# When an attention's value products are issued: one pair of heads at a time, or several pairs together

## The chip, the cores and the metric

The kernel runs on one core of one Trainium2 chip. The metric is the device time in microseconds (us) of one execution. Before the change it is 994.13 us, the median of three runs between 993.94 and 994.28.

## The reference

Two layers of a hybrid decoder work on 256 tokens of width 1024 in float32. Each layer is a gated feed-forward block, a token-mixing block, and a second feed-forward block, each followed by a layer norm of `ALPHA * x + block(x)`. The mixing block projects `x` once, feeds three mixers with the columns (a short convolution, a spatial-gating MLP, and an attention with three branches), and sends the joined results through one output projection. The change touches the attention alone:

```python
# 8 heads of 64 in 2 groups; 256 tokens; three branches with keys and values of their own
o_cmp = softmax(q kc^T, causal on 15 compressed blocks) @ vc
o_s   = softmax(q ks^T, causal) @ vs        # 16 >= 4 blocks: all of them are selected
o_w   = softmax(q kw^T, causal, window 512) @ vw
o     = g0 * o_cmp + g1 * o_s + g2 * o_w    # sigmoid gates per token and head
```

## The kernel before

TensorE products in float32 are split in three: an operand is held as a rounded part ("hi") and a remainder ("lo"), and `hi*hi + hi*lo + lo*hi` is summed in PSUM (`mm3`, L183 to L187, and `proj_chan`, L189 to L197). Weights stream from HBM in blocks of 512 KB and are split on arrival by ScalarE (L162) and VectorE (L163).

The attention part of `mixing` (from L627) goes through twelve steps: four for token tile 0 (128 tokens, one pair of heads each) and eight for token tile 1 (one head each, over 256 keys). A step is
- `scores` (L661 to L674): products of queries and keys of both branches into one PSUM bank, tag `y`, which has 4 slots;
- `attend` (L676 to L702): the maximum (VectorE, L681), the exponentials (ScalarE, L685), their scaling by gate and sum (VectorE, L689 to L692) into a tile `P`, four transposes on TensorE (L696, tile `trp`, tag `tr`, 2 slots), and a copy into `PT` (ScalarE, L698). `P` and `PT` share the tag `a` with 9 slots;
- `values(t, j)` (L704 to L721): for pair `j` of heads, products of the values and `PT` into `o[t]` (L717). `o[t]` is a bank of tag `y` as well. An instruction loads 64 columns of weights (two heads share the 128 output partitions); a float32 product is two instructions, so a pair is 8 of them for tile 0 and 16 for tile 1.

`compressed(t)` (L632 to L659) adds the compressed branch to `o[t]`: eight small instructions (L636, PSUM tile `sc`, tag `tr`), a softmax on VectorE and ScalarE (L641 to L651), a transpose (L653, tile `trc`, tag `tr`), a copy (L655) and 16 instructions of 64 columns (L658), which stand behind the opening products of `values`. `heads_out(t)` (L723) splits the finished `o[t]` into `mixh` and `mixl` for the output projection `w_out`, whose PSUM tiles are `yo`.

Work of the other mixers is written between the steps, to fill TensorE: `conv_h` behind step 0, `spatial` behind step 2 (L570, tile `psv`, also with 64 columns of weights), `conv_c` and `conv_b` behind step 4; `w_out(0)` follows the loop, then `heads_out(1)`, the layer norm of tile 0 and `w_out(1)`.

The order in which it is written is not the order in which it runs. A planner lays out the queue of each engine when the program is compiled: among the instructions that it holds ready at a moment of its own estimate, the one written first goes first, so what is written later fills holes. A tile takes a slot of its tag when the planner places the first instruction that writes it. The engines then work through their queues in that order.

The loop, as it stands before (L734 to L749):

```python
for i, (t, slots) in enumerate(steps):
    if t not in o:
        gates(t)
        o[t] = ps.tile([128, 4, 128], F32, name="o", tag="y", bufs=4)
    for j in range(i and i + 2, min(i + 3, len(steps))):
        sc[j] = scores(*steps[j])
    attend(t, slots, sc.pop(i))
    if slots[-1] % 2:
        values(t, slots[-1] // 2)
    if i in (1, 5):
        compressed(t)
    if i == 3:
        heads_out(0)
    for fn in fill.get(i, []):
        fn()
```

Of the kernel before, what the change touches and what calls it, by code (L numbers as in the profile page):

```python
# [121 lines left out]
def _build(tc, A, out):  # L122
# [3 lines left out]
    with ExitStack() as es:  # L126
# [178 lines left out]
        def layer_norm(t, y, coef, eps, gb, last=False, after=None):  # L305
            g, b = gb
            with tc.high_priority(offset=200):
                st = sm.tile([128, 2, 6], F32, name="st")
                for h in range(2):
                    c = slice(h * 512, h * 512 + 512)  # L310
                    DVE.scalar_tensor_tensor(x[t][:, c], x[t][:, c], coef, y[h], ALU.mult, ALU.add)
                    DVE.bn_stats(st[:, h, :], x[t][:, c])
                mean, rs = rstd_of(st, eps)
                for h in range(2):
                    c = slice(h * 512, h * 512 + 512)
                    DVE.scalar_tensor_tensor(x[t][:, c], x[t][:, c], mean, g[:, c], ALU.subtract, ALU.mult)
                    DVE.scalar_tensor_tensor(x[t][:, c], x[t][:, c], rs, b[:, c], ALU.mult, ALU.add)
                    if last:
                        SP.dma_start(out[t * 128:(t + 1) * 128, c], x[t][:, c])
                    elif after:  # L320
                        with tc.issue_after(after[h].ins):
                            to_xT(t, h)
                    else:
                        to_xT(t, h)
# [121 lines left out]
        def mixing(l, sp):  # L446
# [162 lines left out]
            def w_out(t, kbs, tag, bufs, by_half):  # L609
                w = blocks((l, "wo"))  # L610
                if t not in yo:
                    yo[t] = [ps.tile([128, 512], F32, name="yo", tag=tag, bufs=bufs) for _ in range(2)]
                todo = [(kb, n) for kb in kbs for n in range(2)]
                if by_half:
                    todo.sort(key=lambda v: v[1])
                for kb, n in todo:
                    s = slice(n * 512, n * 512 + 512)
                    mm3(yo[t][n], (mixh[t][:, kb, :], mixl[t][:, kb, :]),
                        (w[kb][0][:, s], w[kb][1][:, s]), kb == 0, kb == 7)
# [7 lines left out]
            def gates(t):  # L627
                e1[t] = sm.tile([128, 3, 8], F32, name="e1")
                ACT.activation(e1[t].rearrange("p a b -> p (a b)"), vv[t][:, 256:280], AF.Exp, scale=-1.0)
                DVE.tensor_scalar(e1[t], e1[t], 1.0, None, op0=ALU.add)  # L630
# [30 lines left out]
            def scores(t, slots):  # L661

                nk = t + 1
                w = nk * 128
                sc = ps.tile([128, 4 // nk, w], F32, name="scm", tag="y", bufs=4)
                for i, s in enumerate(slots):
                    j, g = divmod(s, 2)
                    lq = QS[j // 2][:, j % 2, g, t * 128:t * 128 + 128]
                    dst = sc[:, 2 * i:2 * i + 2, :]
                    PE.matmul(dst, lhsT=lq, rhs=KH[:, g, :, :w], start=i == 0, stop=True, skip_group_check=True)  # L670
                    PE.matmul(dst, lhsT=lq, rhs=KL[:, g, :, :w], start=False, stop=True, skip_group_check=True)
                PE.matmul(sc[:, :, w - 128:], lhsT=identb, rhs=causal[:, :4 // nk, :], start=False, stop=True,
                          skip_group_check=True)
                return sc  # L674

            def attend(t, slots, sc):  # L676
                nk = t + 1
                w = nk * 128
                m = 4 // nk
                nm = sm.tile([128, 4], F32, name="nm")  # L680
                DVE.tensor_reduce(nm[:, :m], sc, AX.X, ALU.max, negate=True)  # L681
                P = wk.tile([128, m, w], F32, name="P", tag="a")
                su = sm.tile([128, 4], F32, name="su")
                for i in range(m):
                    ACT.activation(P[:, i, :], sc[:, i, :], AF.Exp, bias=nm[:, i:i + 1], accum_out=su[:, i:i + 1])  # L685
                h = len(slots)
                suv = su[:, :m].rearrange("p (s b) -> p s b", s=h)
                ev = e1[t][:, 1:3, slots[0]:slots[0] + h].rearrange("p b s -> p s b")
                DVE.tensor_tensor(suv, suv, ev, ALU.mult)  # L689
                DVE.reciprocal(su[:, :m], su[:, :m])  # L690
                for i in range(m):
                    DVE.tensor_scalar(P[:, i, :], P[:, i, :], su[:, i:i + 1], None, op0=ALU.mult)  # L692
                Pv = P.rearrange("p a b -> p (a b)")
                tr = ps.tile([128, 4, 128], F32, name="trp", tag="tr")
                for i in range(4):
                    PE.transpose(tr[:, i, :], Pv[:, i * 128:i * 128 + 128], ident)  # L696
                PT = wk.tile([128, 4, 128], F32, name="PT", tag="a")
                ACT.copy(PT, tr)  # L698
                for si, s in enumerate(slots):
                    for br in range(2):  # L700
                        for kb in range(nk):
                            weights[t, s, br, kb] = PT[:, (si * 2 + br) * nk + kb, :]  # L702

            def values(t, j):  # L704

                with ExitStack() as order:
                    for i in opened.get(t, []):  # L710
                        order.enter_context(tc.issue_after(i.ins))
                    for br in range(2):
                        for kb in range(t + 1):
                            for g in range(2):
                                c0 = br * 128 + g * 64
                                first = len(opened.setdefault(t, [])) < 2
                                i = PE.matmul(o[t][half[g], j, :], lhsT=vv[kb][:, c0:c0 + 64],  # L717
                                              rhs=weights.pop((t, 2 * j + g, br, kb)), start=first, stop=True,
                                              skip_group_check=True)
                                if first:  # L720
                                    opened[t].append(i)  # L721

            def heads_out(t):  # L723
                split_to(mixh[t][:, 4:8, :], mixl[t][:, 4:8, :], o[t])
# [5 lines left out]
            with ExitStack() as order:  # L730
                for i in gelus:
                    order.enter_context(tc.issue_after(i.ins))
                sc = {}
# [4 lines that stand above are left out]
                    for j in range(i and i + 2, min(i + 3, len(steps))):  # L738
                        sc[j] = scores(*steps[j])
                    attend(t, slots, sc.pop(i))  # L740
                    if slots[-1] % 2:
                        values(t, slots[-1] // 2)
                    if i in (1, 5):
                        compressed(t)
                    if i == 3:
                        heads_out(0)
                    for fn in fill.get(i, []):
                        fn()
                w_out(0, range(4), "gu", 2, False)  # L749
                w_out(0, range(4, 8), "gu", 2, True)  # L750
                heads_out(1)
                layer_norm(0, yo[0], ALPHA, EPS, gbn)
                w_out(1, range(8), "y", 4, True)
                layer_norm(1, yo[1], ALPHA, EPS, gbn)

        for l in range(L):
            small = []
            ffn(l, 1, 0, mid=lambda: small.append(load_small(l)))
            mixing(l, small[0])
            ffn(l, 2, 2, last=l == L - 1)  # L760
# [37 lines left out]
```

## Time and profile before

| what | value |
|---|---|
| median of the runs | 994.13 us |
| the profiled execution's own time | 993.1 us |
| its span | 991.4 us |
| TensorE busy (PE) | 978.0 us, 99% |
| weight loads (PEld) | 887.4 us, 90% |
| VectorE busy (DVE) | 603.2 us, 61% |
| ScalarE busy (ACT) | 468.4 us, 47% |
| mean granted TensorE clock | 0.997 of full speed |

The own time of the profiled execution holds 1.7 us outside the span. The attention of the first layer lies at about 238 to 300 us of the span, that of the second at about 726 to 789 us. In a row of the timeline the first number is the start, the second the time until the last of the merged instructions ended; since products overlap in the pipeline, what a product costs is read from the distance of starts, not from its own length.

### The profile page before, as it was taken

How to read it: one execution, taken by the hardware profiler on the slowest of the kernel's cores; microseconds unless marked ns; L12 is line 12 of the kernel's file. 1: busy time of each engine (PE TensorE's matmuls, PEld its weight loads, DVE VectorE, ACT ScalarE, POOL GpSimd, SP SyncE). 2: the span in 40 equal slices, each digit the busy share in tenths (PEclk: the TensorE clock that was granted, in tenths of full speed). 3: DMA queues.
4: the chain of work that ended last, by engine and by line, in shares of the span. 5: the costliest groups of instructions: out<-in, count | busy, mean ns of one | idle time of the engine just before them, and what ended most of it. 6: DMA issues, size and time to landing. Idle time of an engine off the chain costs nothing.

```text
span 991.4 us, 16634 instructions
## 1 busy us (share of the span) xinstructions
PE 978.0 (99%) x6824; PEld 887.4 (90%) x6828; DVE 603.2 (61%) x830; ACT 468.4 (47%) x658; POOL 19.7 (2%) x42
## 2 busy tenths in 40 slices
PE   7999999999999999999999999999999999999996
PEld 6999999899878899999889999998988789999995
DVE  6655455686769555455584545548678785545534
ACT  6644444256655444344354444434565663534420
POOL 1000000010000000000000000000000000000000
PEclk9999999999999999999999999999999999999998
DMA  8967565385226666556375766554642265755601
GB/s 284 331 241 237 171 198 187 105 309 160 87 86 194 231 213 194 189 189 205 94 231 195 255 205 202 196 157 168 237 149 85 86 229 198 253 190 184 205 16 42
DMA packets 53067, 183.17 MB, mean 185 GB/s; under 512 B 6656, under 2 KB 7168, under 8 KB 52992
## 3 DMA queue, kind: packets, MB, share of 16 engines
q1 hardware_dynamic: 52992, 182.12, 55.2%
q8 instruction: 53, 0.87, 0.4%
q14 instruction: 22, 0.18, 0.1%
HBM read 181.05 MB, written 1.05 MB: 184 GB/s over the span
## 4 chain that ended last, share of the span: by engine, by line
PE 99%; DMA 0%; DVE 0%; issue 0%; SPq 0%; DVEq 0%; ACT 0%
PE y L185 8%; PE y L187 8%; PE y L186 8%; PE pu L195 7%; PE pg L195 7%; PE pg L197 7%; PE pu L197 7%; PE pg L196 7%; PE pu L196 7%; PE pc L195 3%; PE pc L197 3%; PE pc L196 3%; PE pg L187 2%; PE yo L187 2%; PE yo L185 2%; PE pg L185 2%
## 5 line engine op out<-in xcount | busy, mean ns | idle before, releaser
L163 DVE TENSOR_TENSOR lo<-raw,hi 128x1024 fp32r<-128x1024 f32 (+2 forms) x326 | 389.9, 1203 | 283.1 <-ACT hi L162 267.3
L162 ACT CAST hi<-raw 128x1024 fp32r<-128x1024 f32 (+2 forms) x326 | 335.1, 1037 | 385.6 <-PE pu L196 153.6
L195 PE MATMUL pu<-xTh,hi 128*128 128x256 f32 x576 | 161.3, 280 | 0.0
L195 PE MATMUL pg<-xTh,hi 128*128 128x256 f32 x576 | 161.3, 280 | 0.0
L197 PE MATMUL pu<-xTh,lo 128*128 128x256 f32 x576 | 160.8, 279 | 0.0
L197 PE MATMUL pg<-xTh,lo 128*128 128x256 f32 x576 | 160.8, 279 | 0.0
L196 PE MATMUL pu<-xTl,hi 128*128 128x256 f32 x576 | 160.8, 279 | 0.0
L196 PE MATMUL pg<-xTl,hi 128*128 128x256 f32 x576 | 160.7, 279 | 0.0
L185 PE MATMUL y<-hi,hTh 128*128 128x512 f32 x352 | 138.6, 394 | 0.0
L187 PE MATMUL y<-hi,hTl 128*128 128x512 f32 x352 | 137.4, 390 | 0.0
L186 PE MATMUL y<-lo,hTh 128*128 128x512 f32 x352 | 136.9, 389 | 0.0
L195 PEld LDWEIGHTS pu<-xTh,hi 128*128 128x128 f32 x576 | 108.1, 188 | 1.1
L196 PEld LDWEIGHTS pu<-xTl,hi 128*128 128x128 f32 x576 | 107.8, 187 | 1.1
L197 PEld LDWEIGHTS pu<-xTh,lo 128*128 128x128 f32 x576 | 108.3, 188 | 0.0
L197 PEld LDWEIGHTS pg<-xTh,lo 128*128 128x128 f32 x576 | 108.3, 188 | 0.0
L195 PEld LDWEIGHTS pg<-xTh,hi 128*128 128x128 f32 x576 | 108.1, 188 | 0.1
L196 PEld LDWEIGHTS pg<-xTl,hi 128*128 128x128 f32 x576 | 107.8, 187 | 0.1
L187 PEld LDWEIGHTS y<-hi,hTl 128*128 128x128 f32 x352 | 66.0, 188 | 14.7
L186 PEld LDWEIGHTS y<-lo,hTh 128*128 128x128 f32 x352 | 66.1, 188 | 12.6
L185 PEld LDWEIGHTS y<-hi,hTh 128*128 128x128 f32 x352 | 66.1, 188 | 12.3
L195 PE MATMUL pc<-xTh,hi 128*128 128x256 f32 x256 | 73.0, 285 | 0.0
L197 PE MATMUL pc<-xTh,lo 128*128 128x256 f32 x256 | 72.5, 283 | 0.0
(153 smaller groups left out, 1246.4 us busy)
## 6 DMA issues: line engine op xcount, KB each, us to landing
raw<-in_ws SPq DMA_DIRECT2D x312, 512.0 KB, 4.6
w<-in_ws SPq DMA_DIRECT2D x8, 512.0 KB, 6.1
lng<-in_ln SPq DMA_DIRECT2D x6, 512.0 KB, 6.7
lnb<-in_ln SPq DMA_DIRECT2D x6, 512.0 KB, 7.5
raw<-in_ws SPq DMA_DIRECT2D x8, 256.0 KB, 4.0
raw<-in_ws SPq DMA_DIRECT2D x4, 420.0 KB, 3.5
x<-in_x SPq DMA_DIRECT2D x4, 256.0 KB, 4.5
out<-x SPq DMA_DIRECT2D x4, 256.0 KB, 2.1
```

What stands on the lines that cost most here:

```text
L162: splits.append((ACT.copy(hi, raw), DVE.tensor_tensor(lo, raw, hi.bitcast(F32), ALU.subtract)))
L163: DVE.tensor_tensor(lo, raw, hi.bitcast(F32), ALU.subtract)))
L185: PE.matmul(o, lhsT=a[0], rhs=b[0], start=start, stop=False)
L186: PE.matmul(o, lhsT=a[0], rhs=b[1], start=False, stop=False)
L187: return PE.matmul(o, lhsT=a[1], rhs=b[0], start=False, stop=stop)
L195: PE.matmul(p[:, b, :], lhsT=hi, rhs=xTh[:, k, :], start=k == 0, stop=False)
L196: PE.matmul(p[:, b, :], lhsT=hi, rhs=xTl[:, k, :], start=False, stop=False)
L197: PE.matmul(p[:, b, :], lhsT=lo, rhs=xTh[:, k, :], start=False, stop=k == KC - 1)
```

## The change

Inside the loop, `values` no longer follows each finished pair. The four pairs of token tile 0 are all issued behind step 3, pairs 0 and 1 of token tile 1 behind step 7, and pairs 2 and 3 behind step 11. `compressed(t)` moves behind them: from step 1 to step 3 for tile 0, from step 5 to step 7 for tile 1. Nothing else changes.

```diff
                     attend(t, slots, sc.pop(i))
-                    if slots[-1] % 2:
-                        values(t, slots[-1] // 2)
-                    if i in (1, 5):
+
+
+                    for j in {3: range(4), 7: range(2), 11: range(2, 4)}.get(i, ()):
+                        values(t, j)
+                    if i in (3, 7):
                         compressed(t)
                     if i == 3:
                         heads_out(0)
```

## Rows read from the trace of the kernel before

**Rows 1.** The page: busy time of the engines; the chain that ended last.

```profile
PE 978.0 (99%) x6824; PEld 887.4 (90%) x6828; DVE 603.2 (61%) x830; ACT 468.4 (47%) x658; POOL 19.7 (2%) x42
...
PE 99%; DMA 0%; DVE 0%; issue 0%; SPq 0%; DVEq 0%; ACT 0%
```

**Rows 2.** Timeline, PE: a pair of tile 0; start, length, engine, line, shape, count.

```profile
255.69 0.28 PE L196 MATMUL pc<-xTl,hi 128*128 128x256 f32 x1
255.90 0.66 PE L717 MATMUL o<-PT,vv 128*64 128x128 f32 x8
...
256.71 0.28 PE L195 MATMUL pc<-xTh,hi 128*128 128x256 f32 x1
```

**Rows 3.** Timeline, PE: compressed branch and a pair of tile 0, back to back.

```profile
260.75 1.09 PE L658 MATMUL o<-pcT,vcb 128*64 128x128 f32 x16
261.68 0.61 PE L717 MATMUL o<-PT,vv 128*64 128x128 f32 x8
```

**Rows 4.** Timeline, PE: the transposes of one step between products of the convolution.

```profile
268.57 0.28 PE L195 MATMUL pc<-xTh,hi 128*128 128x256 f32 x1
268.69 0.60 PE L696 MATMUL trp<-ident,P 128*128 128x128 f32 x4
...
269.25 0.28 PE L197 MATMUL pc<-xTh,lo 128*128 128x256 f32 x1
```

**Rows 5.** Timeline, PE: most of a pair of tile 1 between products of `w_out`.

```profile
290.42 0.40 PE L187 MATMUL yo<-hi,mixl 128*128 128x512 f32 x1
290.74 1.09 PE L717 MATMUL o<-PT,vv 128*64 128x128 f32 x14
...
292.10 0.39 PE L186 MATMUL yo<-lo,mixh 128*128 128x512 f32 x1
292.33 0.39 PE L187 MATMUL yo<-hi,mixl 128*128 128x512 f32 x1
```

**Rows 6.** Timeline, PE: the first two instructions of tile 1's first pair.

```profile
271.76 0.41 PE L696 MATMUL trp<-ident,P 128*128 128x128 f32 x2
272.10 0.43 PE L717 MATMUL o<-PT,vv 128*64 128x128 f32 x2
272.47 0.63 PE L636 MATMUL sc<-kcb,qf 128*128 128x32 f32 x4
```

**Rows 7.** Timeline, PEld: the first weight load behind the pair of rows 2.

```profile
256.49 0.19 PEld L197 LDWEIGHTS pc<-xTh,lo 128*128 128x128 f32 x1 [0.17 <-issue]
```

**Rows 8.** Timeline, PE: the first pair of tile 0, and scores behind it.

```profile
250.87 0.66 PE L717 MATMUL o<-PT,vv 128*64 128x128 f32 x8
251.46 0.38 PE L670 MATMUL scm<-KH,QS 128*128 128x256 f32 x1
```

**Rows 9.** Timeline, ACT: the copy of step 0, and the first exponential of step 1.

```profile
249.75 0.59 ACT L698 COPY PT<-trp 128x512 f32<-128x512 f32 x1 [1.39 <-PE trp L696]
250.23 0.37 ACT L685 ACTIVATE P<-scm,nm 128x128 f32<-128x128 f32 x1
```

**Rows 10.** Timeline, PE: spatial products and step 0's transposes, between two convolution products.

```profile
247.46 0.28 PE L197 MATMUL pc<-xTh,lo 128*128 128x256 f32 x1
...
248.03 0.44 PE L696 MATMUL trp<-ident,P 128*128 128x128 f32 x2
...
249.64 0.87 PE L570 MATMUL psv<-wst,vg 128*64 128x128 f32 x10
...
250.66 0.28 PE L196 MATMUL pc<-xTl,hi 128*128 128x256 f32 x1
```

**Rows 11.** Timeline, DVE: compressed branch of tile 0, first and last; convolution, last two.

```profile
255.22 0.29 DVE L641 TENSOR_TENSOR pcm<-sc,cadd 128x128 f32<-128x128 f32 x1
...
258.93 0.28 DVE L651 TENSOR_TENSOR pcm<-pcm,csum 128x128 f32<-128x128 f32 x1
...
269.49 0.48 DVE L596 SCALAR_TENSOR_TENSOR yc<-z,taps,yc 128x254 f32<-128x254 f32 x1
...
271.53 0.68 DVE L602 TENSOR_TENSOR yc<-yc,pc 128x512 f32<-128x512 f32 x1
```

## The prediction, written before the result

> **What bounds the kernel now.** I read the page first: TensorE is busy for 99% of the span and the chain that ended last is TensorE for 99% too [rows 1]. So a microsecond is won only where TensorE does less, or where its queue loses less between two products; making VectorE or ScalarE faster, or their steps earlier, is worth nothing unless TensorE stands still for them. Then I read TensorE's timeline through the attention of layer 1. It has no long idle stretch: low-priority products fill every hole. But starts are not evenly spaced. Where an instruction with 64 weight columns (L717, L658, L570) follows one with 128, and again on the way back, starts come later than the stream's rhythm. That toll is what the change can lower. The same code runs once per layer, so everything below counts twice.
>
> **The price of a switch.** Products of the convolution start 0.12 us apart (268.57 to 268.69) [rows 4]. Behind the one at 255.69 the next two were due at 255.81 and 255.93; the second came at 256.71 [rows 2]. So a group of eight costs 0.78 us. Sixteen instructions of the kind take 261.68 - 260.75 = 0.93, or 0.058 each, and a further group of the same shape behind them pays no toll [rows 3]; eight are 0.46, and 0.32 is the switch. Between products of `w_out`, 0.23 apart, fourteen cost 292.10 - 290.88 = 1.22 (due: 290.42 + 2 x 0.23), less 0.81: 0.41 [rows 5]. Two instructions between transposes and small scores cost 272.47 - 271.76 - 2 x 0.058 = 0.59, less 0.12: 0.47 [rows 6]. A switch there and back is 0.32 to 0.47 us. Four transposes, which have 128 columns, cost 269.25 - 268.81 = 0.44 with a toll of only 0.21 [rows 4].
>
> [...]
>
> **What the change does to the order.** Written order is not queue order, so first the groups before, counted along the timeline of a layer: tile 0 has four (8, 8, 16+8 with the compressed branch, 8), tile 1 eight (2, 14, 16+2, 14, 2, 14, 2, 14). Tile 1's pairs are split because the first product needs only the first head's `PT`, and the planner issues it at once. This is the weak point of the change: `values` is still written ahead of `conv_c`, `conv_b` and `w_out`, which fill TensorE at that time, so a ready pair still goes before them, alone. Written together is not issued together.
>
> One thing holds the pairs back: the PSUM slot of `o[t]`. Tiles of one tag get their slots in the order of their first instructions. Two rows show it. The scores of step 3 start at 251.46, right behind the first pair [rows 8], although step 0's score bank was free before its transposes began at 248.03 [rows 10] and although products of lower priority ran meanwhile: `o[0]`, first written by that pair, stood ahead of them. And the exponentials of step 1 start at 250.23, right behind the copy of step 0 [rows 9], though ScalarE had idled 1.39 us before that copy: `PT` is ahead of the next `P`. Behind the change `o[0]` is first written behind step 3, so the scores of steps 3, 4 and 5 take their slots first, and `o[0]` gets that of step 2, when step 2's exponentials end. These follow the copy of step 1. By then pairs 0 and 1 are ready and go as one group of 16; pairs 2 and 3 and the compressed branch come one after another: 16, 8, 8, 16, again four groups. `o[1]` now stands behind the scores of step 9 and gets its slot behind the exponentials of step 6: both heads of pair 0 are ready then, so its split goes: 16, 2, 14, 16+2, 14, 2, 14, seven groups for eight.
>
> **The sum.**
> - Tile 1, one switch less, the one at 272.10: -0.47 a layer [rows 6]. Bounds: -0.32 (the cheapest row) to -0.94 (if one more pair closes up), nothing if the slot comes early. I take the row of that group itself.
> - Tile 0, value groups: none. Bounds: 0.32 either way, for one group more or less.
> - Scores of step 3 are free of `o[0]` now and stand right behind `conv_h`, those of step 4 behind them: both before `spatial` in priority. Before, `spatial` stepped in there while the scaled pieces of `P` arrived: four groups of `psv` and three of transposes alternate between 247.46 and 250.66 [rows 10]. Those 20 instructions cost 250.66 - 247.70 = 2.96 us. In one piece `psv` would cost 0.32 + 0.93 = 1.25 and the transposes 0.44: 1.69, or 1.27 less. I let the transposes stay in three pieces among the scores, 2 x 0.21 more: -0.85 a layer. Bounds: 0 (all as before) and -1.27. I take -0.85 because the scores, being written earlier, must go first.
> - `compressed` moved: same instructions on all engines, no DMA and nothing on POOL or SP. Its chain on VectorE ran 3.99 us from first to last [rows 11]; it now stands in the queue behind step 3 instead of step 1, so the wait of the next step's transposes for the shared slots of `tr` moves from step 2 to step 4 and from step 6 to step 8. TensorE fills it with convolution and `w_out` products: 0. Without that cover it costs up to the third rival's price.
> - `o[0]` finishes later, and `heads_out(0)` with it; its reader, the second half of `w_out(0)`, stands behind 24 products of the first half (24 x 0.23 = 5.5 us [rows 5]): 0. Up to four `PT` are held longer, of 9 slots: 0. The added wait of the first pairs for a slot leaves nothing standing behind it as long as the planner's estimate of that moment holds.
>
> Sum: (-0.47 - 0.85) x 2 = -2.6 us. The profiled execution, 993.1, would become 990.5; it lies 1.0 below the median of the runs, so the median goes from 994.13 to 991.5. The bounds of this case alone: -0.6 (0.32 x 2) to -4.4 ((0.94 + 1.27) x 2), so 989.7 to 993.5.
>
> **The rivals.**
> 1. Nothing to measure, 993.9. `psv` stays cut up because the pieces of `P` and not the scores decide, and only half the gain of tile 1 comes: -0.2 us. For it: the planner goes by readiness, and readiness is set by ScalarE and VectorE, which the change leaves alone. Against it: the two slot rows.
> 2. The change does what it says: groups of 32, 16 for tile 0 and 32, 16, 32 for tile 1, five for twelve. Two switches of 0.32 and five of 0.41 are 2.7 a layer; with `spatial` 3.55, so -7.1 and 987.0. For it: the more the slot is late in the plan, the more pairs close up. Against it: pairs 2 and 3 are ready one by one and ahead of all fill.
> 3. Slower: the compressed branch of tile 0 now falls on VectorE into the stretch where the convolution is made ready for `w_out`. Its last step before the final product ended at 269.97, that product began at 271.53 [rows 11]: 1.56 us of slack against 3.99 of chain. If the whole chain gets in ahead, `w_out(0)` starts 2.4 us later with no other fill left: 4.9 in two layers, less the 2.6, +2.3: 996.4. It decides from the point where the inserted work exceeds 1.56 us. For it: VectorE's instructions in that chain have the higher priority. Against it: steps 2 and 3 lose the same chain and so run earlier.
> [...]
>
> **How the numbers follow.** Chances: forecast 0.45, rival 1 0.27, rival 2 0.12, rival 3 0.13, rival 4 0.03. About 0.2%, 2 us, is what a measurement can tell from no change here. Faster by more than that: three quarters of the forecast (0.34), rival 2 (0.12) and a little of rival 1 (0.03): 0.49. Slower: nearly all of rival 3: 0.12. The rest, 0.39, is no change. The range reaches to half of rival 2 below and short of rival 3 above: 987.5 to 995.8.
>
> **What would show it.** Right: in the changed trace the scores of step 3 directly behind `conv_h`; `psv` in one run of 16; a first L717 group of 16 in each tile; eleven groups of 64-column instructions in place of twelve; TensorE's granted clock and its instruction count as before. Wrong: L717 in runs of 32; or `psv` still alternating with `trp`; or TensorE idle between the last convolution product and the first `yo`, with VectorE's L602 late.

## The result, and the profile after

The changed kernel takes 1004.48 us, the median of four runs from 1004.11 to 1004.77, against 994.2 for the kernel before in the same job: a ratio of 1.0103, 95% interval 1.009 to 1.0115. It is slower by 10.3 us, where 2.6 us less was forecast. The profiled execution took 1004.11 us with a span of 1002.4, 11.0 above that of before.

Read the page first, as before: its busy row and its chain answer to [rows 1].

```profile
PE 979.6 (98%) x6824; PEld 890.9 (89%) x6828; DVE 602.1 (60%) x830; ACT 467.2 (47%) x658; POOL 19.7 (2%) x42
...
PE 96%; ACT 1%; DVE 1%; issue 1%; DMA 0%; SPq 0%; DVEq 0%; ACTq 0%
```

The instruction counts are the same and TensorE works hardly longer (979.6 for 978.0), but the chain that ended last now runs through ScalarE and VectorE too: TensorE waits. The table of windows says where. Its columns are the window, its length, each engine's busy time with instruction counts, TensorE's granted clock, the DMA share and GB/s. First the attention of layer 1 with what stands around it in the kernel before, then the same window of the changed kernel, then the changed kernel cut finer.

```profile
238.00:330.00 92.00, 91.81 (x632) 74.58 (x627) 73.73 (x159) 57.47 (x126) 1.91 (x2) 1.00 0.41 129
```

```profile
238.00:330.00 92.00, 87.50 (x618) 72.17 (x619) 69.68 (x157) 52.67 (x122) 1.91 (x2) 0.98 0.37 124
```

```profile
238.00:300.00 62.00, 61.59 (x493) 51.34 (x494) 49.23 (x128) 37.72 (x101) 0.92 (x1) 1.00 0.33 107
300.00:311.00 11.00, 6.91 (x41) 5.23 (x40) 6.63 (x11) 6.00 (x12) 0.00 (x0) 0.84 0.58 192
311.00:330.00 19.00, 19.00 (x88) 15.60 (x87) 13.81 (x20) 8.95 (x10) 0.99 (x1) 1.00 0.41 139
```

TensorE was idle for 0.19 us of these 92 and is now idle for 4.50, of which 4.09 fall into 11 us at the end of the attention. There the granted clock has a mean of 0.84: it is 0.50 of full speed from 305.00 to 308.42 us, and 1.00 in the rest of those 11 us. The list of TensorE's waits over the whole span names the releasers (columns: total us, times, longest):

```profile
PE trp L696 <- DVE P L692: 6.1, 2, 3.0
...
PE o L717 <- ACT PT L698: 2.0, 2, 1.0
PE yo L185 <- ACT mixh L200: 0.7, 2, 0.3
```

Each comes twice, once a layer. The rest of this section is layer 1.

TensorE's timeline, where it stands still:

```profile
299.99 0.60 PE L696 MATMUL trp<-ident,P 128*128 128x128 f32 x4
300.35 0.48 PE L187 MATMUL yo<-hi,mixl 128*128 128x512 f32 x1
301.85 0.43 PE L717 MATMUL o<-PT,vv 128*64 128x128 f32 x2 [1.02 <-ACT PT L698]
305.32 0.45 PE L696 MATMUL trp<-ident,P 128*128 128x128 f32 x1 [3.04 <-DVE P L692]
305.56 1.06 PE L217 MATMUL tr<-ident,x 128*128 128x128 f32 x4
...
309.13 1.09 PE L717 MATMUL o<-PT,vv 128*64 128x128 f32 x14
```

The first row holds the transposes of step 10 (the steps count from 0; 11 is the last). The product at 300.35 is the last `yo` that can run: 72 have gone, the 48 of `w_out(0)` and the 24 of `w_out(1)` that read no attention. The other 24 need `o[1]`, and `o[1]` needs steps 10 and 11. So TensorE waits 1.02 us for the copy of step 10 and 3.04 us for the scaled `P` of step 11. In the kernel before, 57 had gone ahead of step 11's transposes: it had fill left.

VectorE in the same place, in the changed kernel:

```profile
296.29 0.11 DVE L690 RECIPROCAL su<-su 128x2 f32<-128x2 f32 x1
...
296.47 1.41 DVE L316 SCALAR_TENSOR_TENSOR x<-x,mv,lng 128x512 f32<-128x512 f32 x2
297.80 1.41 DVE L317 SCALAR_TENSOR_TENSOR x<-x,rs,lnb 128x512 f32<-128x512 f32 x2
299.12 0.61 DVE L692 TENSOR_SCALAR P<-P,su 128x256 f32<-128x256 f32 x2
299.65 3.49 DVE L163 TENSOR_TENSOR lo<-raw,hi 128x1024 fp32r<-128x1024 f32 x3
303.05 0.15 DVE L689 TENSOR_TENSOR su<-su,e 128x2 f32<-128x2 f32 x1
303.24 0.17 DVE L690 RECIPROCAL su<-su 128x2 f32<-128x2 f32 x1
303.69 1.23 DVE L163 TENSOR_TENSOR lo<-raw,hi 128x1024 fp32r<-128x1024 f32 x1 [0.28 <-ACT hi L162]
304.83 0.61 DVE L692 TENSOR_SCALAR P<-P,su 128x256 f32<-128x256 f32 x2
```

The factor for step 10's scaling is there at 296.40 (296.29 + 0.11). The scaling (L692) starts at 299.12: between them stands the second half of the layer norm of tile 0 (L316, L317), 2.65 us that nobody waits for yet. In the kernel before the same norm stood behind the last scaling:

```profile
297.18 0.34 DVE L692 TENSOR_SCALAR P<-P,su 128x256 f32<-128x256 f32 x1
...
297.55 0.30 DVE L692 TENSOR_SCALAR P<-P,su 128x256 f32<-128x256 f32 x1
...
297.83 1.40 DVE L316 SCALAR_TENSOR_TENSOR x<-x,mv,lng 128x512 f32<-128x512 f32 x2
```

These are step 11's scalings, a whole step further on. And ScalarE after:

```profile
298.37 2.95 ACT L162 CAST hi<-raw 128x1024 fp32r<-128x1024 f32 x3 [2.89 <-PE yo L187]
301.23 0.57 ACT L698 COPY PT<-trp 128x512 f32<-128x512 f32 x1
301.70 0.47 ACT L685 ACTIVATE P<-scm,nm 128x256 f32<-128x256 f32 x1
```

Read the three timelines as one chain. Step 10's scaling is late (299.12), its transposes with it (299.99); its copy to `PT` then finds three weight splits ahead of it and starts at 301.23; the exponentials of step 11 stand behind that copy (301.70); their sum stands behind three splits on VectorE (303.05), and its scaling behind one more (304.83). Each step hangs on the one before, so a delay is carried through to the end.

### The profile page after: what moved, and what is told of

Its sections match the earlier page's. It is cut to its first block, busy times and chain, and to the rows that moved or that the text cites. A ratio compares the mean times of both kernels' runs of the same rounds, so it can differ in the third digit from the quotient of the medians.

```text
span 1002.4 us, 16628 instructions
## 1 busy us (share of the span) xinstructions
PE 979.6 (98%) x6824; PEld 890.9 (89%) x6828; DVE 602.1 (60%) x830; ACT 467.2 (47%) x658; POOL 19.7 (2%) x42
## 3 DMA queue, kind: packets, MB, share of 16 engines
HBM read 181.05 MB, written 1.05 MB: 182 GB/s over the span
## 4 chain that ended last, share of the span: by engine, by line
PE 96%; ACT 1%; DVE 1%; issue 1%; DMA 0%; SPq 0%; DVEq 0%; ACTq 0%
PE y L185 8%; PE y L187 8%; PE y L186 8%; PE pg L195 7%; PE pu L195 7%; PE pu L197 7%; PE pg L197 7%; PE pu L196 7%; PE pg L196 7%; PE pc L195 3%; PE pc L197 3%; PE pc L196 3%; PE pg L185 2%; PE pg L187 2%; PE pg L186 2%; PE pu L185 2%
```

## The experiments

Theory A: the loss comes from the compressed branch of tile 0 behind step 3. The last steps come later against the products of `w_out`; a norm written to run 200 instructions ahead then overtakes their scaling; the fill is used up. Its rivals were that the batching of the values itself costs (slots of `P` and `PT` held longer, pairs late), and that the compressed branch of tile 1 does it. All ratios are to the kernel before in the same job, with 95% intervals.

**The compressed branch of tile 0 alone.** The pairs stay as before, one at a time.

```diff
-                    if i in (1, 5):
+                    if i in (3, 5):
```

> The kernel before with one edit: the compressed branch of tile 0 behind step 3 instead of step 1; all pairs where they were. Theory A (the late compressed branch delays the last attention steps, the layer norm of tile 0 overtakes them, and TensorE has no product left to fill with): this edit alone loses much of the 10 us, 998 to 1005 us. Theory B (the batched pairs and the later slot of o are the cause): no change, 993 to 995 us.

Measured: 1005.37 us, 1.0115 (1.0099 to 1.0132): the whole loss, without any batching. TensorE waits as in the changed kernel, and VectorE's timeline has the same block in the same place:

```profile
PE trp L696 <- DVE P L692: 6.1, 2, 3.0
```

```profile
296.99 1.41 DVE L316 SCALAR_TENSOR_TENSOR x<-x,mv,lng 128x512 f32<-128x512 f32 x2
...
299.63 0.61 DVE L692 TENSOR_SCALAR P<-P,su 128x256 f32<-128x256 f32 x2
```

**The compressed branch of tile 1 alone.**

```diff
-                    if i in (1, 5):
+                    if i in (1, 7):
```

> The kernel before with one edit: the compressed branch of tile 1 behind step 7 instead of step 5. Theory A: slower too, 996 to 1003 us, since steps 8 to 11 come later against w_out. Theory B: no change, 993 to 995 us.

Measured: 995.95 us, 1.0023 (1.0013 to 1.0034). It costs some 2 us, and not through an empty fill: 62 of the 72 products have gone ahead of step 11's transposes, and TensorE waits for neither `P` nor `PT`. The norm's second half stands between the two scalings of step 11 here (299.18 and 302.11), and TensorE waits 0.8 us a layer for `xTh`, the norm's result split for the next block. This branch isn't the cause of the ten microseconds.

**Pairs written together, the branches not moved.**

```diff
-                    if slots[-1] % 2:
-                        values(t, slots[-1] // 2)
+                    for j in {1: range(2), 3: range(2, 4), 5: (0,), 7: (1,), 11: range(2, 4)}.get(i, ()):
+                        values(t, j)
                     if i in (1, 5):
```

> Pairs batched (0 and 1 behind step 1, 2 and 3 behind step 3; of tile 1 pairs 2 and 3 behind step 11) with the compressed branch left behind steps 1 and 5. Theory A: the loss is gone or nearly so, 991 to 997 us (the spatial products in fewer pieces are worth 1 to 2 us, and part of step 11 may still stand behind the layer norm). Theory B: about as slow as the changed kernel, 1002 to 1005 us.

Measured: 994.11 us, 0.9999 (0.999 to 1.0008). This says less than it seems. The planner still issues the pairs of tile 0 one at a time (8, 8, 16, 8, 8, the 16 being the compressed branch); only `psv` goes from four pieces to two, 6 and 10, with the first pair between them. That leaves 13 groups of 64-column instructions in a layer's attention where the kernel before has 16 (`psv` counted), and still nothing is gained: TensorE now waits 0.4 us a layer for `mixh` and 0.2 for a slot of the scores. Writing pairs together does no harm, but here it doesn't join them either.

**The norm without its priority, in the changed kernel.**

```diff
-                layer_norm(0, yo[0], ALPHA, EPS, gbn)
+                layer_norm(0, yo[0], ALPHA, EPS, gbn, ahead=0)
```

`ahead` is a new argument, the offset of the norm's priority; it is 200 in every other call.

> The changed kernel, with the layer norm of tile 0 in the mixing block at its written place instead of 200 instructions ahead. Theory A: VectorE's 2.65 us of the norm and what follows leave the way of steps 10 and 11, half of the loss or more comes back: 995 to 1000 us. Theory B: no change, 1003 to 1006 us. If the norm's priority alone is the cause (theory C): at or below the kernel before, 990 to 994 us.

Measured: 994.93 us, 1.0009 (0.9999 to 1.0018): nine tenths of the loss are gone with one number. The waits that stay are those of a fill that is still used up (72 products ahead of step 11), and they are short:

```profile
PE trp L696 <- DVE P L692: 1.3, 2, 0.7
PE o L717 <- ACT PT L698: 1.3, 2, 0.6
```

So an empty fill leaves 1.3 us of waiting a layer here; what made it 4 was the norm in front. Even the 1.3 is no fixed price of an empty fill: in the runs with only the norm's second half behind (below) the 72 products are gone ahead of step 11 too, and TensorE waits 0.24 us there.

**Which half of the norm.** The norm is cut in two priority blocks: statistics (L310 to L312, `rstd_of`) and application (L316, L317, transposes). One run has the second half behind, the other the first.

```diff
-            with tc.high_priority(offset=200):
+            with tc.high_priority(offset=early):
...
+            with tc.high_priority(offset=ahead):
```

`early` stands over the statistics and `ahead` over the application. Both are 200 in every call but that for tile 0 in mixing, where the first run has `ahead` at 0 and the second `early`.

> The changed kernel; of the norm of tile 0 in the mixing block the sums and statistics stay 200 instructions ahead, its second half (four VectorE instructions of 0.7 us, the transposes and their copies) is left at its written place. If that second half is what overtakes step 10: 994 to 997 us, as with the whole norm behind. If the first half (taking the sums out of PSUM early) is what does the harm: 1002 to 1005 us.

> The mirror of it: sums and statistics at their written place, second half still 200 ahead. If the second half does the harm: most of it stays, since step 11 still stands behind it in part, 998 to 1004 us. If the first half does: 994 to 996 us.

Measured: second half behind, 995.1 us, 1.0016 (1.0007 to 1.0025); first half behind, 998.59 us, 1.0046 (1.0032 to 1.0059). With the statistics late, L317 waits for the last of them (`rs`, 0.73 us) and moves behind step 10's scaling too, while L316 stays ahead of it: TensorE's wait for `P` is 2.1 us over both layers instead of 6.1. The application is what overtakes. Both runs carried a cost of the cut itself, which the last pair of runs shows.

**The kernel before, norm without its priority.** The edit is that of the fourth run, on the kernel before.

> The kernel before, with the norm of tile 0 in the mixing block at its written place. There the last scaling of the attention already ran ahead of the norm's second half, so nothing is in the way: no change within 1 us, 993.2 to 995.2 us. If the norm's priority costs by itself, wherever the attention stands: 988 to 992 us.

Measured: 994.65 us, 1.0005 (0.9996 to 1.0013). The priority is worth nothing there, and harms nothing: it takes the late compressed branch to make it harmful.

**Pairs 0 and 1 together behind step 1, the branches not moved, norm 60 ahead.** A try for a version that beats the kernel before.

```diff
+                    for j in {1: range(2), 2: (2,), 3: (3,), 5: (0,), 7: (1,), 9: (2,), 11: (3,)}.get(i, ()):
+                        values(t, j)
...
+                layer_norm(0, yo[0], ALPHA, EPS, gbn, ahead=60)
```

> A candidate: pairs 0 and 1 of tile 0 together behind step 1, all else and the compressed branch as before the change, and the norm 60 instead of 200 instructions ahead. It keeps the spatial products in two pieces instead of four, and the attention ends ahead of the norm. By the tolls of the prediction 1 to 3 us faster than before: 991 to 993 us. If waits eat the tolls, as with the pairs batched and the norm at 200: 993.5 to 995 us.

Measured: 994.07 us, 1.0001 (0.9992 to 1.001). The groups of tile 0 are those of the third run (pairs written together, the branches not moved), 13 in all, with the same two waits: no gain.

**Late compressed branch of tile 0, pairs singly, norm behind.** The first and the fourth edit together, on the kernel before.

> Pairs as in the kernel before, one at a time; the compressed branch of tile 0 behind step 3, which alone gave 1005.4; and the norm of tile 0 without its priority. Theory A (the loss is the meeting of the late compressed branch with a norm that overtakes the scaling of steps 10 and 11 on VectorE; it has nothing to do with batching): the loss goes as it did in the changed kernel, 994 to 996, TensorE waits under 0.5 us for each step's P at the end, granted clock of the last stretch at full. Rival (the norm's priority matters only with the values batched, since only then the last steps come together): it stays at 1003 to 1006.

Measured: 997.91 us, 1.0035 (1.0021 to 1.0048). Some 8 of the 11 us are back without any batching, so the rival fell; but theory A's 994 to 996 was missed too, and its waits of under 0.5 us are 0.6 and 0.7. TensorE's list of waits has the same two rows as the fourth run (the changed kernel, norm without its priority), 1.3 us in two times each. With the same waits it is 0.26% slower than the fourth run, and the intervals stand apart. The two differ in the pairs (and in the compressed branch of tile 1, which by the second run is no help to the fourth). Counted along layer 1's timeline, this run has 17 groups of 64-column instructions in the attention (`psv` four, values and compressed branch thirteen) and the fourth has 12. In the table below the stages differ by 1.9 and 1.8 us a layer. Most of that is the toll that the change was to save. An estimate from the starts in the traces: take the instructions that enter or leave such a group, waits left out, and add up how much further apart they start than the instruction ahead takes in its own stream (0.23, 0.12 and 0.06 us for 512, 256 and 128 columns out). In layer 1 that is 4.7 us for the 17 groups of this run and 3.1 for the 12 of the fourth. It is 4.3 for the 16 groups of the kernel before and 3.3 for the 12 of the changed kernel.

**Compressed branch of tile 1 and its first two pairs as before, second half of the norm behind.**

```diff
-                    for j in {3: range(4), 7: range(2), 11: range(2, 4)}.get(i, ()):
+                    for j in {3: range(4), 5: (0,), 7: (1,), 11: range(2, 4)}.get(i, ()):
                         values(t, j)
-                    if i in (3, 7):
+                    if i in (3, 5):
```

> The changed kernel with pairs 0 and 1 of tile 1 one at a time and its compressed branch back behind step 5 (late it cost 2.3 us by itself), and with the norm's second half written in its place. If the two costs are apart and add: 995.1 less up to 2.3, 992.8 to 994, the one version so far that could beat the kernel before. If the norm's second half, once behind, gives the slack for both: 995, no gain. If the tolls saved always come back as waits: 994 to 995.

Measured: 999.03 us, 1.0046 (1.0033 to 1.0058), outside all three expectations. What the second run cost is not won back here: with everything else of the change in place, tile 1 is better in the changed order. Against the run with the second half behind (the first of the two with the cut norms), this one has a group more, 13 for 12, and TensorE's waits at the end are 1.3 us a layer instead of 0.25. Of the 5 us, 2.5 lie in the two stages (table below), and 1.0 in the stretch between, where it has the cut norms.

**The cut of the norms.** One run takes the second half of the norm out of the priority for tile 0 in mixing alone, and leaves every other norm in one block. The other cuts all norms of the kernel before in two blocks and moves nothing.

```diff
+        def layer_norm(t, y, coef, eps, gb, last=False, after=None, behind=False):
             g, b = gb
             with tc.high_priority(offset=200):
...
+                if not behind:
+                    apply(t, mean, rs, g, b, last, after)
+            if behind:
+                apply(t, mean, rs, g, b, last, after)
```

`apply` holds the second half, and `behind` is set in the call for tile 0 in mixing.

> The changed kernel with the second half of the norm of tile 0 in mixing written in its place, as in the run that gave 995.1, but with every other norm of the kernel left in one prioritised piece. In the 995.1 run the two attention stages were 85.45 and 85.43 us (86.05 and 86.11 in the kernel before), yet the stretch between the layers was 403.0 (402.0 before, 401.4 in the changed kernel) and that ahead of the first attention 233.2 (230.9 and 231.7). Theory A with that side effect (cutting the other norms in two places cost the gain): the stages stay at 85.4, the stretch between returns to 401.4, and the time is 991.5 to 993, faster than both kernels. Rival (the stretches are longer because of what the attention leaves behind it, or by chance of the start): 995, as in that run.

> The kernel before with every norm's two halves under a priority of their own, both 200 instructions ahead, and nothing moved. Side effect as supposed: the stretch between the layers is about 403 instead of 402.0, the first stretch up to 1 us longer, the attention stages 86.0 to 86.2, in all 995 to 997. Rival (cutting costs nothing): 994.1.

Measured: the change with the second half behind, 991.73 us (990.58 to 992.31, seven runs), 0.9975 (0.9964 to 0.9986): faster than both kernels, by 2.2 and 12.7 us. The kernel before with cut norms: 996.78 us, 1.0029 (1.0019 to 1.0039). The cut alone costs 2.8 us, so the runs with the cut in every norm had looked that much worse than their attention was. VectorE, TensorE and the window of the attention in the faster kernel, where the chain stood (here L322 and L323 are the norm's second half, L698 is the scaling, L702 the transposes, L704 the copy and L723 the values):

```profile
296.45 0.74 DVE L322 SCALAR_TENSOR_TENSOR x<-x,mv,lng 128x512 f32<-128x512 f32 x1
297.11 0.61 DVE L698 TENSOR_SCALAR P<-P,su 128x256 f32<-128x256 f32 x2
297.79 0.75 DVE L323 SCALAR_TENSOR_TENSOR x<-x,rs,lnb 128x512 f32<-128x512 f32 x1
...
300.50 0.62 DVE L698 TENSOR_SCALAR P<-P,su 128x256 f32<-128x256 f32 x2
```

```profile
301.68 0.60 PE L217 MATMUL tr<-ident,x 128*128 128x128 f32 x4
302.52 1.09 PE L723 MATMUL o<-PT,vv 128*64 128x128 f32 x14 [0.24 <-ACT PT L704]
```

```profile
238.00:330.00 92.00, 91.30 (x642) 75.25 (x643) 74.23 (x161) 56.86 (x127) 2.07 (x2) 1.00 0.41 133
```

The scaling at 297.11 is that of step 10, now behind only one of the norm's four instructions and 2.0 us earlier than in the changed kernel (whose attention starts 0.2 us later); its copy on ScalarE starts at 298.56, 2.7 us earlier and ahead of the weight splits; step 11 is scaled 4.3 us earlier. TensorE is idle for 0.70 us of the 92, and its granted clock stays at 1.00. The kernel before with only that half of the norm behind was not run; with the whole norm behind it stands at 1.0005.

**All runs in one table.** A stage is the time on TensorE from the first L504 (the second compression ahead of the attention) to the sixtieth product of the feed-forward behind it, by the starts in the trace; "between" is the time from the end of layer 1's stage to the start of layer 2's. Us of one profiled execution each.

```
                                            layer 1  between  layer 2   ratio
before                                        86.05   402.02    86.11   1
changed kernel                                90.26   401.39    91.92   1.0103
compressed 0 late                             91.78   401.39    91.34   1.0115
compressed 1 late                             87.17   402.01    87.22   1.0023
written together, branches not moved          86.08   402.38    86.14   0.9999
changed, norm behind                          86.21   401.42    86.36   1.0009
changed, 2nd half behind, all norms cut       85.45   403.01    85.43   1.0016
changed, 1st half behind, all norms cut       86.99   403.03    87.03   1.0046
before, norm behind                           86.09   401.99    86.09   1.0005
compressed 0 late, norm behind                88.13   401.99    88.18   1.0035
tile 1 back, 2nd half behind, all norms cut   87.34   403.01    87.37   1.0046
changed, 2nd half behind in mixing alone      85.00   402.02    84.97   0.9975
pairs 0 and 1 together, norm 60 ahead         86.10   401.99    86.07   1.0001
before, all norms cut                         86.38   402.96    86.19   1.0029
```

The two stages of the changed kernel are 4.2 and 5.8 us longer: 10.0 of the 11.0 in the spans. The stretch between is 0.6 shorter, and the first attention starts 1.6 us later in this execution (237.8 to 239.4 us): 0.9 of it is a longer wait for `x` at the very start, which the edit can't reach.

The loss as a table of two by two, in us against the kernel before, each ratio less 1, times 994:

| | norm 200 ahead | norm behind |
|---|---|---|
| pairs and branches as before | 0 | +0.5 |
| compressed branch of tile 0 late | +11.4 | +3.5 |
| the whole change | +10.2 | +0.9 |

The late branch costs 3 us by itself; its meeting with the norm's priority costs about 8 more; the rest of the change gives 1.2 (the intervals overlap) to 2.6 back.

## Why the prediction was wrong, point by point

**The order: right in all that was named.** These rows of the changed kernel's TensorE timeline are the ones that the prediction named:

```profile
248.97 0.28 PE L670 MATMUL scm<-KH,QS 128*128 128x256 f32 x1
...
250.85 1.09 PE L570 MATMUL psv<-wst,vg 128*64 128x128 f32 x16
...
256.90 1.09 PE L717 MATMUL o<-PT,vv 128*64 128x128 f32 x16
...
272.91 0.50 PE L185 MATMUL yo<-hi,mixh 128*128 128x512 f32 x1 [0.33 <-ACT mixh L200]
...
278.06 1.09 PE L717 MATMUL o<-PT,vv 128*64 128x128 f32 x16
```

Step 3's scores stand right behind `conv_h`; `psv` is in one run of 16, where it had four pieces [rows 10], each tile's first value group has 16, and the layer has 11 groups of values and compressed branch: 16, 8, 8, 16 and 16, 2, 14, 16+2, 14, 2, 14. The reading of slots [rows 8, 9] held.

**The sum of the tolls: right in size.** The forecast was 1.32 us a layer. With the late loss taken away, the stages are 1.05 and 1.14 us shorter than before (85.00 and 84.97), and the time 2.2 us lower, for 2.6 forecast. In the changed kernel itself the gain is there and is buried: by the estimate above its switches cost 1.0 us less in layer 1 than those of the kernel before (3.3 for 4.3). It is a gain only where no wait takes it back: the run with the pairs written together has 13 groups for 16 and gains nothing.

**The step that failed: "`compressed` moved ... TensorE fills it with convolution and `w_out` products: 0."** The fill was there where the move was made, and was then missing at the end. It is a fixed stock: 72 products of `w_out` can run before the last heads are done. I read the cover at the place of the edit and not whether it lasts to the last step that needs it. In the changed kernel it was used up at 300.35, with step 11 five microseconds away. The term was put at nothing; the run with the branch of tile 0 alone puts it at 11.4 us, of which 3 are left when the norm's priority is gone.

**How the fill ran out.** Count from the first L504, at 237.78 before and 239.39 after. The first `yo` comes at 36.4 us before (274.14) and at 33.5 after (272.91): the products that fill start 2.8 us earlier. The transposes of step 9 come at 51.5 before (289.30) and at 53.4 after (292.83): 1.9 us later. So 47 products have gone ahead of them instead of 32. TensorE's rows, first of the kernel before, then of the changed one, then of the run with the branch of tile 0 alone late:

```profile
274.14 0.48 PE L185 MATMUL yo<-hi,mixh 128*128 128x512 f32 x1
...
289.30 0.60 PE L696 MATMUL trp<-ident,P 128*128 128x128 f32 x4
```

```profile
292.83 0.60 PE L696 MATMUL trp<-ident,P 128*128 128x128 f32 x4
```

```profile
275.80 0.47 PE L185 MATMUL yo<-hi,mixh 128*128 128x512 f32 x1
...
293.88 0.60 PE L696 MATMUL trp<-ident,P 128*128 128x128 f32 x4
```

The last of the three tells which of the two matters. Its first L504 is at 238.92, so its first `yo` comes at 36.9, half a microsecond later than before, and step 9 at 55.0, 3.4 later; 45 products have gone, and the loss is whole. The lateness of the steps is enough; the early start of the fill isn't needed. In that run steps 2 to 4 come 1.3 to 2.2 us earlier than before and all from step 5 on later, by 1.6 us at first. At step 5, VectorE has the split of `o[0]` (now later), the convolution and a weight split between the step's sum (270.68) and its scaling (274.14).

Another part of the lateness is in VectorE's rows ahead of step 9's sum (L689), first of the kernel before, then of the changed one:

```profile
286.89 1.22 DVE L163 TENSOR_TENSOR lo<-raw,hi 128x1024 fp32r<-128x1024 f32 x1
288.30 0.16 DVE L689 TENSOR_TENSOR su<-su,e 128x2 f32<-128x2 f32 x1 [0.18 <-ACT P L685]
```

```profile
288.14 2.35 DVE L163 TENSOR_TENSOR lo<-raw,hi 128x1024 fp32r<-128x1024 f32 x2
290.49 0.69 DVE L311 SCALAR_TENSOR_TENSOR x<-x,yo 128x512 f32<-128x512 f32 x1
291.10 0.15 DVE L689 TENSOR_TENSOR su<-su,e 128x2 f32<-128x2 f32 x1
```

The planner put two weight splits there instead of one, and the first instruction of the norm. From there the norm is ahead of the steps, and its second half meets step 10. The run with the branch of tile 0 alone has the two splits there as well (289.21), without earlier products; what lets the second one in stays open.

The prediction's sentence that earlier steps on VectorE or ScalarE are "worth nothing unless TensorE stands still for them" [rows 1] was right for the kernel before. The change is what made TensorE stand still, and I never asked what a later step would meet in VectorE's queue: the layer norm is not named anywhere in the prediction.

**Rival 3 named the culprit, in the wrong place and at less than half of the price.** It had the compressed branch of tile 0 delaying `w_out(0)` by 2.4 us a layer, 4.9 in all, for 996.4; that branch alone costs 11.4. The wait there is 0.33 us (the row at 272.91), and the first `yo` starts earlier than before, as said. The loss came 30 us later, and the range, which stopped at 995.8, was set by that rival's place. The argument against it ("steps 2 and 3 lose the same chain and so run earlier") came true, by 2.2 and 1.9 us in the run with that branch alone, and was no help: from step 5 on the steps are late.

**Rivals 1, 2 and 4.** `psv` did close up, so the first fell; runs of 32 don't appear, so the second fell; the quarter of a percent between 17 groups and 12 with equal waits, and the 4.7 and 3.1 us that their switches add up to, speak against the fourth, switches that cost nothing (0.03 among the chances).

**The clock.** "TensorE's granted clock and its instruction count as before": the count is (6824 in both), the clock isn't: it fell to 0.50 at 305.00 and at 796.52, in both layers while TensorE stood waiting for step 11's `P`, 2.7 and 2.4 us after its last product had ended.

## What to carry to other kernels

When work is moved within planned queues, don't only ask what hides it where it lands: follow the stock of low-priority work to the last instruction that depends on the moved work, and list what holds a higher priority on the other engines there. A priority that costs nothing today (0.05% here, within its interval) can cost 0.8% after an edit somewhere else, so a small regression after a reordering is worth one run with the neighbouring priorities taken away before the edit is given up. And change a priority at one call: cutting a block in every call to test it in one place cost 2.8 us of its own, hid a gain in one run and made two more look worse than they were.

## What the runs showed of the hardware that was not expected

After the two waits TensorE's products run at about half pace for a while. The four `tr` transposes at 305.56 took 1.06 us, and 0.60 us in the faster version (301.68). In layer 2 of the changed kernel products with 512 columns out start 0.43 us apart in that stretch (799.72 and 800.15), for 0.23 ahead of the waits (790.91 and 791.14), and the fourteen products of the last pair fell into it as well:

```profile
801.56 1.94 PE L717 MATMUL o<-PT,vv 128*64 128x128 f32 x14
```

They took 1.09 us in layer 1. The stage of layer 2 is 1.7 us longer than that of layer 1 though its two waits are the same 3.0 and 1.0 us. The granted clock is at 0.50 for longer there, 6.8 us (796.52 to 803.35) against 3.4 us in layer 1 (305.00 to 308.42): its mean is 0.84 in the 11 us from 300.0 and 0.70 in the 11 us from 792.2, the same place in layer 2. So these idle stretches cost more than their own length, and not the same in both layers; why the clock stays down longer in layer 2 isn't shown. In the faster version, with TensorE idle for 0.70 us of the 92, the granted clock has a mean of 1.00.

VectorE's queue showed no way round a waiting instruction in one place of the changed kernel. At 303.41 the factor of step 11's scaling was ready; ahead of the scaling stood a weight split, which itself waited 0.28 us for ScalarE and then took 1.14, and the scaling started at 304.83.
